# Head norms' sums spread over column tiles, the sparse branch ahead of the memory's, the diagonal first among the level scores, and 38 column tiles computed with 512-column matmuls

## The chip, the cores and the metric

The kernel runs on one core of a Trainium2 chip. The metric is the device time of one execution in microseconds (us), the median of several runs. Every time below is from the profiled execution of the kernel before, unless it is called a run's time.

## The reference

Two transformer blocks follow each other on one sequence of 256 tokens of width 1024, all in float32. Cut to the order of its steps:

```python
# block 1
h = rms_norm(x, norm_mix); proj = h @ w_in             # stick-breaking heads, GLA heads, gates
o_sb = stick_breaking_attention(sb_q, sb_k, sb_v)
o_gla = gla_chunked(g_q, g_k, g_v, log_a)              # gated linear attention, chunks of 64
x = x + (sigmoid(gate_sb) * (o_sb @ w_proj_sb) + sigmoid(gate_gla) * (o_gla @ w_proj_gla)) @ w_out
x = x + square(relu(rms_norm(x, norm_mlp) @ w_ff1)) @ w_ff2
# block 2
proj = rms_norm_2(x, norm_mix_2) @ w_in_2
q, k_s, k_w, qm = (rms_norm_2 of every head)           # the head norms
o_nsa = nsa_attention(...)                             # compressed, selected and window keys
o_m = softmax(qm @ km) @ vm                            # a memory of 256 frames
u = silu(layer_norm(conv31(a * sigmoid(ag))))
merged = g0 * (o_nsa @ w_nsa_out) + g1 * (u @ w_conv_out) + g2 * (o_m @ w_mem_out)
h = x + merged @ w_out_2
out = h + (silu(hn @ w_gate) * (hn @ w_up)) @ w_down   # hn = rms_norm_2(h, norm_ffn_2)
```

## The kernel before

Activations lie transposed: 128 features on the partitions, 256 tokens along a row. A product with a weight matrix goes over *column tiles* of 128 output features and, within one, over *K tiles* of 128 input features; `kt` is the number of K tiles. For float32 accuracy weights and activations are each split into a high and a low half of a type that TensorE takes, and a product is hi·h + hi·l + lo·h (weight half first).

`Stream.prepare` brings eight weight tiles at a time: one 512 KB DMA on SP's queue into `raw` (4 buffers), a cast to `hi` on ACT (L520), a subtraction to `lo` on DVE (L522), with three buffers each for `hi` and `lo`.

`steps_b` (L278) computes column tiles in one of two ways. A *plain* pair of tiles takes for every K tile three matmuls of 256 columns (L324 hi·h, L326 hi·l, L328 lo·h; L308 to L310 are the same for the pair that leads a matrix). A *joint* tile uses that h and l of a K tile lie side by side: for every K tile one matmul of 512 columns gives hi·[h|l] (L295) and one of 256 columns adds lo·h (L296). It fills both halves of a PSUM bank alone, and what evacuates it, called with c = 0, must add the halves. In this kernel wf2, wdn (7 of 8 tiles each) and 40 of the 44 tiles of wgu2 are joint; wgu2's `evf` copies one half on ACT (L1179) and adds the other on DVE (L1180) into `ffr`, and works on a pair at every second tile. wo1, wf1, wo2 and the projections are plain. `residual` (wo1, wo2) adds a tile to x on DVE (L551), splits it (ACT L429, DVE L430) and sums its squares (ACT L462, POOL L469). `evf` of wf1 takes max and scale on DVE (L691), the square on ACT (L693) and splits the result into halves (ACT L426, DVE L427).

Four other places matter.

- `gla_scores` (L744) computes scores within chunks by levels of halving width. In three pairs, six batches of 64 matmuls of 32x32 (L822) are issued: five from a `level` tile `lev` (made on DVE, ACT, DVE, L791 to L794) and, sixth, the diagonal, straight from `gq` and `gk`. A mask per level multiplies them on DVE (L825). They run inside the plain tiles of w1a and the projection `gemm_a` (L367).
- `block_two` (L1043) writes PE's order by hand in a `manual_schedule` (L1098 to L1130). There `compress` (matmuls L1229, L1239, L1258, L1266), `nsa_operands` and the gate column tiles (`fill(gates, ...)`) are generators stepped in turn. `nsa_operands` (L1300) squares the head vectors ksw, q and qm on ACT (L1310) and sums each over a head by matmuls against a column or two of ones (L1313, forty, all in its first step), then makes 1/sqrt by Ln (L1292), Exp (L1293) and one Newton step (L1294 to L1296) and spreads it over rows by matmuls (L1328).
- `w2v` follows as a `gemm_a`: 48 matmuls of 256 columns on L367.
- The branches (L1147 to L1160) run in the order memory (wmo), sparse attention (wno), convolution (wco). Each evacuation multiplies by its gate (L1151) and adds into the gate tiles `gm[4..5]`: branch 0 on POOL, branch 1 on DVE (L1153).

Of the kernel before, what the change touches and what calls it, by code (L numbers as in the profile page):

```python
# [446 lines left out]

class Squares:
# [97 lines left out]
def residual(K, x, H, gain, sqs):  # L546
    nc = K.nc

    def ev(i, c, ps):
        d = x[i // 4][:, (i % 4) * 256:(i % 4 + c) * 256]  # L550
        nc.vector.tensor_tensor(d, ps.rearrange("p a t -> p (a t)"), d, op=OP.add)  # L551
        for j in range(c):
            K.split(H.h(i + j), H.l(i + j), d[:, j * 256:j * 256 + 256], gain[:, i + j:i + j + 1])
        sqs.add(d)
    return ev


def block_one(K, B, after):
# [125 lines left out]
    K.gemm_b(K.stream("wo1"), 8, 8, M, residual(K, x1, X1, par["norm_mlp"], sqs1), lead=nothing, single=2)  # L684
# [11 lines left out]
    K.gemm_b(K.stream("wf1"), 8, 32, X1, evf, lead=lambda: r1.append(K.rms(sqs1.parts(), D, EPS, "rr")[1]))  # L696
# [47 lines left out]
def gla_scores(K, c, gq, gk):  # L744
# [64 lines left out]
    for pr in range(3):  # L809
        ps = K.pt().rearrange("p (l i h t) -> p l i h t", l=2, i=2, h=4)  # L810
        for j in range(2):
            l = 2 * pr + j
# [11 lines left out]
        for j in range(2):  # L824
            nc.vector.tensor_tensor(m[:, j * 256:j * 256 + 256].rearrange("p (a t) -> p a t", t=32),  # L825
                                    ps[:, j].rearrange("p i h t -> p (i h) t"), bc(lv[:, 2 * pr + j], 8), op=OP.mult)
# [216 lines left out]
def block_two(K, B, KM, vm, out):  # L1043
# [54 lines left out]
    with tc.manual_schedule(engines={mybir.EngineType.PE}):  # L1098
# [3 lines left out]
        for _ in range(6):  # L1102
            next(cmp)
            fill(heads, 1)
# [6 lines left out]
        fill(gates, 2)  # L1111
        next(cmp)
        pre = nsa_operands(K, N, B.eps)
# [33 lines left out]
    def branch(n):  # L1147
        def ev(i, c, ps):
            d = slice((i % 4) * 256, (i % 4 + c) * 256)
            g_, t = gm[2 * n + i // 4][:, d], gm[4 + i // 4][:, d]  # L1150
            nc.vector.tensor_tensor(g_, ps.rearrange("p a t -> p (a t)"), g_, op=OP.mult)  # L1151
            if n != 2:
                (nc.vector if n == 1 else nc.gpsimd).tensor_tensor(t, t, g_, op=OP.add)  # L1153
            if n == 1:
                K.split(M.h(i, c), M.l(i, c), t)
        return ev

    K.gemm_b(K.stream("wmo"), 4, 8, OM, branch(2))
    K.gemm_b(K.stream("wno"), 4, 8, ON, branch(0))
# [3 lines left out]
    K.gemm_b(K.stream("wo2"), 8, 8, M, residual(K, B.x, XF, par["norm_ffn"], sqs), lead=nothing, single=2)  # L1163
# [136 lines left out]
def nsa_operands(K, N, eps):  # L1300
# [6 lines left out]
    for x, n, rhs, m in ((ksw, 2, con["mean64"][:, ::64], 2), (q, 4, con["mean64"][:, ::64], 2),  # L1307
# [3 lines left out]
        for t in range(2):  # L1311
            for i in range(n):
                mm(sums[:, t, at + i * m:at + i * m + m], lhsT=sq[:, i * 256 + t * 128:i * 256 + t * 128 + 128],  # L1313
                   rhs=rhs, start=True, stop=True)
        at += n * m
    v, y, w = (K.small(n, [128, 32], bufs=1) for n in ("hn_v", "hn_y", "hn_w"))
# [291 lines left out]
```

## Time and profile before

| what | value |
|---|---|
| runs | 918.21, 918.55, 919.99 us; median 918.55 us |
| profiled execution | 920.02 us, its span 918.2 us |
| mean granted clock of TensorE | 0.991 of full speed |
| busy share: PE, DVE, ACT, POOL | 98%, 74%, 53%, 6% |
| chain that ended last | 94% on PE |
| DMA | 155.64 MB, mean 170 GB/s; 512 KB weights land after about 3.7 us |

The span is the time between the first and the last instruction of the profile. A matmul's end is modelled, so that rates are read from the starts of rows that follow each other: the timeline joins equal instructions and gives the first start, and the next row's start tells when the engine went on.

### The profile page before, as it was taken

The page shows a single profiled execution, that of the slowest core. Times are in us where ns is not written, and L with a number is a line of the kernel's source. Part 1 is how long each engine was busy: PE and PEld are TensorE (multiplying, and loading weights), DVE is VectorE, ACT ScalarE, POOL GpSimd, SP SyncE. Part 2 cuts the span into 40 slices and gives each one's busy share as a digit, 9 for nine tenths or more (in the row PEclk, how much of TensorE's full clock was granted, in tenths as well). Part 3 has the DMA queues.
Part 4 walks back from the last instruction along what each step waited for, and adds up shares of the span by engine and source line. Part 5 has one row for each costly group of instructions (what it writes and reads, how often), then busy time and mean ns, then how long its engine had stood idle before and what let it go on. Part 6 is the DMA issues. An engine that isn't in the chain of part 4 may idle for free.

```text
span 918.2 us, 17035 instructions
## 1 busy us (share of the span) xinstructions
PE 900.6 (98%) x6818; PEld 828.4 (90%) x6818; DVE 675.6 (74%) x1169; ACT 491.1 (53%) x747; POOL 51.1 (6%) x82
## 2 busy tenths in 40 slices
PE   8998999999999999999999999899999999999998
PEld 6987689999999999888899988799999988888887
DVE  6996768866677666555557986899988788888653
ACT  6653764654456555444444434667854565555432
POOL 1000001210020000001120000000003200000000
PEclk9999999999999999999999998999999999999999
DMA  7643426765666666555656762343445566666672
GB/s 274 202 138 117 115 70 184 228 196 174 195 194 196 180 185 186 173 173 185 189 165 186 225 224 75 95 136 118 116 135 164 184 189 186 191 189 185 193 204 64
DMA packets 45727, 155.64 MB, mean 170 GB/s; under 512 B 5200, under 2 KB 6736, under 8 KB 45648
## 3 DMA queue, kind: packets, MB, share of 16 engines
q1 hardware_dynamic: 45216, 153.48, 54.7%
q8 instruction: 53, 0.87, 0.4%
q10 hardware_dynamic: 432, 1.08, 0.4%
q14 instruction: 26, 0.21, 0.1%
HBM read 153.49 MB, written 1.05 MB: 168 GB/s over the span
## 4 chain that ended last, share of the span: by engine, by line
PE 94%; DVE 3%; issue 1%; ACT 1%; DMA 0%; SPq 0%; DVEq 0%
PE pj L295 18%; PE pj L324 17%; PE pj L326 16%; PE pj L328 16%; PE pj L296 9%; PE pj L367 6%; DVE lo L522 1%; PE pj L309 1%; PE pj L310 1%; PE pj L308 1%; ACT hi L520 1%; PE pt L913 1%; PE pt L1313 1%; PE pt L403 1%; PE pt L1229 1%
## 5 line engine op out<-in xcount | busy, mean ns | idle before, releaser
L520 ACT CAST hi<-raw 128x1024 fp32r<-128x1024 f32 (+1 forms) x278 | 288.6, 1041 | 315.7 <-PE pj L326 133.7
L522 DVE TENSOR_TENSOR lo<-raw,hi 128x1024 fp32r<-128x1024 f32 (+1 forms) x278 | 341.3, 1230 | 105.4 <-ACT hi L520 93.4
L295 PE MATMUL pj<-hid,hi 128*128 128x512 f32 x378 | 134.3, 400 | 0.0
L295 PE MATMUL pj<-xf,hi 128*128 128x512 f32 x320 | 113.2, 399 | 0.0
L296 PE MATMUL pj<-hid,lo 128*128 128x256 f32 x378 | 106.2, 281 | 0.0
L296 PE MATMUL pj<-xf,lo 128*128 128x256 f32 x320 | 89.8, 281 | 0.0
L295 PEld LDWEIGHTS pj<-hid,hi 128*128 128x128 f32 x378 | 71.0, 188 | 17.4
L295 PEld LDWEIGHTS pj<-xf,hi 128*128 128x128 f32 x320 | 60.1, 188 | 14.9
L296 PEld LDWEIGHTS pj<-hid,lo 128*128 128x128 f32 x378 | 71.4, 189 | 0.0
L296 PEld LDWEIGHTS pj<-xf,lo 128*128 128x128 f32 x320 | 60.4, 189 | 0.0
L1536 DVE SCALAR_TENSOR_TENSOR cv<-u,par,cv 128x256 f32<-128x256 f32 x120 | 53.2, 479 | 0.7
L324 PE MATMUL pj<-xm,hi 128*128 128x256 f32 x336 | 50.9, 294 | 0.0
L324 PEld LDWEIGHTS pj<-xm,hi 128*128 128x128 f32 x336 | 44.2, 193 | 5.0 <-ACT hi L520 2.5
L326 PE MATMUL pj<-xm,hi 128*128 128x256 f32 x336 | 47.9, 286 | 0.0
L328 PE MATMUL pj<-xm,lo 128*128 128x256 f32 x336 | 47.2, 283 | 0.0
L328 PE MATMUL pj<-xn,lo 128*128 128x256 f32 x304 | 44.8, 286 | 0.0
L469 POOL TENSOR_TENSOR acc<-acc,ffr 128x256 f32<-128x256 f32 (+1 forms) x25 | 27.3, 1103 | 310.4 <-ACT ffr L462 288.9
L326 PEld LDWEIGHTS pj<-xm,hi 128*128 128x128 f32 x336 | 44.1, 195 | 0.0
L326 PE MATMUL pj<-xn,hi 128*128 128x256 f32 x304 | 44.0, 285 | 0.0
L324 PE MATMUL pj<-xn,hi 128*128 128x256 f32 x304 | 43.8, 285 | 0.0
L328 PEld LDWEIGHTS pj<-xm,lo 128*128 128x128 f32 x336 | 43.5, 193 | 0.0
L328 PEld LDWEIGHTS pj<-xn,lo 128*128 128x128 f32 x304 | 39.7, 192 | 0.5 <-issue 0.4
(471 smaller groups left out, 1632.0 us busy)
## 6 DMA issues: line engine op xcount, KB each, us to landing
raw<-in_wf_dram SPq DMA_DIRECT2D x64, 512.0 KB, 3.7
raw<-in_wgu_dram SPq DMA_DIRECT2D x44, 512.0 KB, 3.7
raw<-in_w1g_dram SPq DMA_DIRECT2D x24, 512.0 KB, 3.8
raw<-in_w2g_dram SPq DMA_DIRECT2D x24, 512.0 KB, 3.7
raw<-in_wdn_dram SPq DMA_DIRECT2D x22, 512.0 KB, 3.9
raw<-in_w2a_dram SPq DMA_DIRECT2D x20, 512.0 KB, 3.7
raw<-in_wo_dram SPq DMA_DIRECT2D x16, 512.0 KB, 3.8
raw<-in_w1a_dram SPq DMA_DIRECT2D x14, 512.0 KB, 3.8
```

What stands on the lines that cost most here:

```text
L295: mm(ps, lhsT=st.hi(w), rhs=x.both(k), start=k == 0, stop=False, skip_group_check=True)
L296: mm(ps[:, :T], lhsT=st.lo(w), rhs=x.h(k), start=False, stop=k == kt - 1, skip_group_check=True)
L308: mm(ps[:, j], lhsT=st.hi(w), rhs=x.h(k), start=k + j == 0, stop=False, skip_group_check=True)
L309: mm(ps[:, j], lhsT=st.hi(w), rhs=x.l(k), start=False, stop=False, skip_group_check=True)
L324: mm(ps[:, j], lhsT=st.hi(o + k), rhs=x.h(k), start=k == 0, stop=False)
L326: mm(ps[:, j], lhsT=st.hi(o + k), rhs=x.l(k), start=False, stop=False)
L328: mm(ps[:, j], lhsT=st.lo(o + k), rhs=x.h(k), start=False, stop=k == kt - 1)
L367: mm(pss[t], lhsT=xx(k)[:, t * 128:t * 128 + 128], rhs=ww(o + k), start=k == 0 and xx == x.h and ww == st.hi, stop=k == kt - 1 and ww == s ...
L469: self.engine.tensor_tensor(a, a, s, op=OP.add)
L520: nc.scalar.copy(hi[:, o:o + n], raw[:, o:o + n])
L522: nc.vector.tensor_tensor(lo[:, o:o + n], raw[:, o:o + n], hi[:, o:o + n].bitcast(F32), op=OP.subtract)
L1536: nc.vector.scalar_tensor_tensor(o, u[:, c, k:k + 256], w[:, c, k:k + 1], o, op0=OP.mult, op1=OP.add)
```

## The change

Four edits.

1. wo1 and wo2 (tiles 2 to 6) and wf1 (tiles 2 to 29) become joint: 5 + 5 + 28 = 38 column tiles with 8 K tiles each. wf1's evacuation is wrapped in the new class `Added`; `residual` adds both halves to x, one after the other.
2. In `gla_scores` the diagonal (number 5) becomes the first of the six batches.
3. `nsa_operands` is created ahead of the compression and yields within its sums, so that they are issued in five lots of eight matmuls: after the second, fourth and sixth step of the compression loop, between the first two gate tiles, and at the old place. What follows the sums keeps its place in the code.
4. The branches run in the order wno, wmo, wco; the sums are kept in `gm[0..1]`; branch 0 only multiplies, and branches 2 and 1 add on DVE. POOL adds nothing here any more.

```diff
+class Added:
+    def __init__(self, k, ev):
+        self.k, self.ev = k, ev
+
+    def __call__(self, i, c, ps):
+        if c:
+            return self.ev(i, c, ps)
+        if i % 2 == 0:
+            self.z = self.k.gsmall("ffr", [128, 512]).rearrange("p (a t) -> p a t", a=2)
+        o = self.z[:, i % 2]
+        self.k.nc.scalar.copy(o, ps[:, 1])
+        self.k.nc.vector.tensor_tensor(o, ps[:, 0], o, op=OP.add)
+        if i % 2:
+            self.ev(i - 1, 2, self.z)
...
     def ev(i, c, ps):
+        parts, c = (2, 1) if c == 0 else (1, c)
         d = x[i // 4][:, (i % 4) * 256:(i % 4 + c) * 256]
-        nc.vector.tensor_tensor(d, ps.rearrange("p a t -> p (a t)"), d, op=OP.add)
+        for j in range(parts):
+            nc.vector.tensor_tensor(d, ps[:, j * c:(j + 1) * c].rearrange("p a t -> p (a t)"), d, op=OP.add)
...
-    K.gemm_b(K.stream("wo1"), 8, 8, M, residual(...), lead=nothing, single=2)
+    K.gemm_b(K.stream("wo1"), 8, 8, M, residual(...), lead=nothing, single=2, joint=range(2, 7))
...
-    K.gemm_b(K.stream("wf1"), 8, 32, X1, evf, lead=...)
+    K.gemm_b(K.stream("wf1"), 8, 32, X1, Added(K, evf), joint=range(2, 30), lead=...)
...
-            l = 2 * pr + j
+            l = (5, 0, 1, 2, 3, 4)[2 * pr + j]
...
         cmp = compress(K, kc2, N)
-        for _ in range(6):
+        pre = nsa_operands(K, N, B.eps)
+        for i in range(6):
             next(cmp)
+            if i in (1, 3, 5):
+                next(pre)
             fill(heads, 1)
...
-        fill(gates, 2)
+        fill(gates, 1)
+        next(pre)
+        fill(gates, 1)
         next(cmp)
-        pre = nsa_operands(K, N, B.eps)
         next(pre)
...
-            g_, t = gm[2 * n + i // 4][:, d], gm[4 + i // 4][:, d]
+            g_, t = gm[2 * n + i // 4][:, d], gm[i // 4][:, d]
             nc.vector.tensor_tensor(g_, ps.rearrange("p a t -> p (a t)"), g_, op=OP.mult)
-            if n != 2:
-                (nc.vector if n == 1 else nc.gpsimd).tensor_tensor(t, t, g_, op=OP.add)
+            if n:
+                nc.vector.tensor_tensor(t, t, g_, op=OP.add)
...
+    K.gemm_b(K.stream("wno"), 4, 8, ON, branch(0))
     K.gemm_b(K.stream("wmo"), 4, 8, OM, branch(2))
-    K.gemm_b(K.stream("wno"), 4, 8, ON, branch(0))
     K.gemm_b(K.stream("wco"), 4, 8, UC, branch(1), single=2)
...
# nsa_operands, in the loop over the sums
+            if n == 4 and t == 0:
+                yield
         at += n * m
+        if at < 16:
+            yield
```

The list of instructions shows what a scheduler and the pools make of it. In the fences below a row is one instruction or several alike: line, operation, out<-in, shape, count; the numbers behind the names tell tiles apart.

The first place is PE in `gla_scores`. Before, the last two batches (the second of them the diagonal, from gq and gk) stand directly behind each other, within `gemm_a`:

```order
L822 MATMUL pt_619<-lev_658 32x32 x32
L328 MATMUL pj_965<-xn_118,lo_999 128x256
L367 MATMUL pj_1027<-hi_1031,xn_115 128x512 x4
L367 MATMUL pj_1027<-lo_1032,xn_115 128x512 x2
L367 MATMUL pj_1027<-hi_1049,xn_116 128x512 x4
L367 MATMUL pj_1027<-lo_1050,xn_116 128x512
L367 MATMUL pj_1028<-hi_1031,xn_115 128x512 x4
L367 MATMUL pj_1028<-lo_1032,xn_115 128x512 x2
L367 MATMUL pj_1028<-hi_1049,xn_116 128x512 x3
L822 MATMUL pt_700<-lev_701 32x32 x32
L822 MATMUL pt_700<-gq_147,gk_148 32x32 x32
L367 MATMUL pj_1028<-hi_1049,xn_116 128x512
```

After (L822 is now L844, L804 now L826), the diagonal stands early, behind the first half of the matmuls for the 32-wide level:

```order
L326 MATMUL pj_841<-xn_118,hi_874 128x256
L826 MATMUL pt_520<-lev_514 32x32 x8
L844 MATMUL pt_539<-gq_147,gk_148 32x32 x32
L326 MATMUL pj_841<-xn_118,hi_874 128x256
L328 MATMUL pj_841<-xn_115,lo_875 128x256 x2
L826 MATMUL pt_520<-lev_514 32x32 x8
L328 MATMUL pj_841<-xn_116,lo_875 128x256 x2
L328 MATMUL pj_841<-xn_117,lo_875 128x256 x2
L328 MATMUL pj_841<-xn_118,lo_875 128x256 x2
L324 MATMUL pj_903<-xn_115,hi_906 128x256 x2
L844 MATMUL pt_539<-lev_572 32x32 x32
```

The diagonal's batch moved ahead of all five others; the level batches follow it, the third and the fourth of them two matmuls apart, and the last one stands alone within `gemm_a`.

The second place is PE ahead of w2v. Before, all forty sums (L1313) stand together, in front of w2v (L367):

```order
L328 MATMUL pj_6042<-xm_4415,lo_6076 128x256 x2
L1239 MATMUL pt_6104<-con,P_874_6040 128x2x15 x4
L1313 MATMUL pt_6120<-con,hsq_6121 128x2 x4
L1313 MATMUL pt_6120<-con,hsq_6127 128x2 x8
L1313 MATMUL pt_6120<-con,hsq_6137 128x1 x8
L1117 MATMUL pt_6157<-con,glow_5255 128x24 x2
L367 MATMUL pj_6166<-hi_6170,xm_4412 128x256
```

After (L1239 is now L1267, L1313 now L1341, L1117 now L1144):

```order
L328 MATMUL pj_5894<-xm_4249,lo_5934 128x256 x2
L328 MATMUL pj_5894<-xm_4250,lo_5934 128x256 x2
L1267 MATMUL pt_5962<-con,P_909_5892 128x2x15 x4
L1341 MATMUL pt_5651<-con,hsq_5925 128x1 x4
L1144 MATMUL pt_5992<-con,glow_5090 128x24 x2
L367 MATMUL pj_6001<-hi_6005,xm_4247 128x256
```

Eight of the sums stay in front of w2v; the other four lots of eight now stand between plain tiles ahead of it. ACT at the same place before (L1292 is the Ln on the sums, L1293 the Exp, L520 the casts of weights):

```order
L1234 COPY P_874_6040<-pt_5759 128x512
L520 CAST hi_6200<-raw_6198 128x1024
L520 CAST hi_6280<-raw_6278 128x1024
L520 CAST hi_6325<-raw_6323 128x1024
L1292 ACTIVATE hn_w_6149<-hn_v_6147 128x32
L1284 ACTIVATE gate_6160<-gate_6160 128x48
L1284 ACTIVATE cmp_t_6111<-cmp_t_6111 128x128
L1293 ACTIVATE hn_y_6148<-hn_w_6149 128x32
L520 CAST hi_6384<-raw_6382 128x1024
```

And after (Ln is now L1320, Exp L1321, the casts L538):

```order
L1262 COPY P_909_5892<-pt_5594 128x512
L538 CAST hi_6035<-raw_6033 128x1024
L538 CAST hi_6115<-raw_6113 128x1024
L1320 ACTIVATE hn_w_5984<-hn_v_5982 128x32
L1321 ACTIVATE hn_y_5983<-hn_w_5984 128x32
L1312 ACTIVATE gate_5995<-gate_5995 128x48
L1312 ACTIVATE cmp_t_5969<-cmp_t_5969 128x128
L538 CAST hi_6160<-raw_6158 128x1024
L538 CAST hi_6219<-raw_6217 128x1024
```

One cast fewer stands between the copy and the Ln, and both functions of the head norms are ahead of the third cast.

## Rows read from the trace of the kernel before

**Rows 1.** Page: busy time by engine, the instruction queue, the chain by engine.

```profile
PE 900.6 (98%) x6818; PEld 828.4 (90%) x6818; DVE 675.6 (74%) x1169; ACT 491.1 (53%) x747; POOL 51.1 (6%) x82
...
q8 instruction: 53, 0.87, 0.4%
...
PE 94%; DVE 3%; issue 1%; ACT 1%; DMA 0%; SPq 0%; DVEq 0%
```

**Rows 2.** Timeline of PE in wf1, plain: start, length, instruction, count.

```profile
299.98 1.12 PE L324 MATMUL pj<-x1n,hi 128*128 128x256 f32 x8
...
302.86 1.12 PE L324 MATMUL pj<-x1n,hi 128*128 128x256 f32 x8
```

**Rows 3.** Timeline of PE in wf2, joint.

```profile
393.23 0.40 PE L295 MATMUL pj<-hid,hi 128*128 128x512 f32 x1
...
396.05 0.40 PE L295 MATMUL pj<-hid,hi 128*128 128x512 f32 x1
```

**Rows 4.** Busy time of stretches (wgu2): us, busy by engine, clock, DMA.

```profile
740.00:850.00 110.00, 110.00 (x633) 95.77 (x633) 90.03 (x140) 65.45 (x121) 0.00 (x0) 1.00 0.62 186
```

**Rows 5.** Timeline of DVE in wf1: the first step of a pair's evacuation.

```profile
300.18 0.69 DVE L691 SCALAR_TENSOR_TENSOR ffr<-pj,rr 128x512 f32<-128x512 f32 x1 [1.53 <-PE pj L328]
```

**Rows 6.** Timeline of DVE in wo2: one column tile evacuated alone.

```profile
724.21 0.42 DVE L551 TENSOR_TENSOR x<-pj,x 128x256 f32<-128x256 f32 x1 [0.27 <-PE pj L328]
724.55 1.64 DVE L522 TENSOR_TENSOR lo<-raw,hi 128x1024 fp32r<-128x1024 f32 x1
726.11 0.97 DVE L430 SCALAR_TENSOR_TENSOR xf<-x,par,xf 128x256 fp32r<-128x256 f32 x1
```

**Rows 7.** Timeline of PE in the level scores: two gaps within batches, the projection behind.

```profile
68.51 0.25 PE L822 MATMUL pt<-lev 128*32 128x32 f32 x3 [0.51 <-issue]
...
76.88 0.41 PE L822 MATMUL pt<-gq,gk 128*32 128x32 f32 x25 [2.23 <-issue]
...
78.25 3.39 PE L367 MATMUL pj<-hi,xn 128*128 128x512 f32 x8
81.44 0.85 PE L367 MATMUL pj<-lo,xn 128*128 128x512 f32 x2
```

**Rows 8.** Stretches with the granted clock behind the busy times (columns as Rows 4).

```profile
78.50:82.00 3.50, 3.50 (x10) 2.73 (x9) 3.13 (x6) 0.67 (x2) 0.00 (x0) 0.51 0.25 50
...
546.00:549.50 3.50, 3.50 (x35) 3.50 (x33) 2.63 (x5) 0.49 (x1) 0.00 (x0) 1.00 0.56 150
549.50:559.80 10.30, 10.30 (x50) 10.30 (x51) 2.17 (x10) 1.63 (x5) 0.00 (x0) 0.50 0.13 51
```

**Rows 9.** Timeline of PE around the sums and w2v.

```profile
547.01 6.38 PE L1313 MATMUL pt<-con,hsq 128*128 128x2 f32 x40
553.25 1.03 PE L1117 MATMUL pt<-con,glow 128*128 128x24 f32 x4
554.10 3.76 PE L367 MATMUL pj<-hi,xm 128*128 128x256 f32 x16
...
564.59 0.42 PE L1258 MATMUL pt<-cmp_h,par 128*64 128x16 f32 x8 [2.02 <-DVE hn_y L1296]
```

**Rows 10.** Timelines of ACT and DVE in the same stretch.

```profile
557.90 1.04 ACT L520 CAST hi<-raw 128x1024 fp32r<-128x1024 f32 x1 [11.41 <-PE pj L367]
558.85 0.23 ACT L1292 ACTIVATE hn_w<-hn_v 128x32 f32<-128x32 f32 x1
...
563.02 1.22 DVE L522 TENSOR_TENSOR lo<-raw,hi 128x1024 fp32r<-128x1024 f32 x1 [0.54 <-ACT hi L520]
```

**Rows 11.** Timeline of PE where the compressed keys are scored.

```profile
578.31 1.94 PE L1366 MATMUL pt<-cmp_kn,q 128*128 128x32 f32 x16 [0.46 <-DVE nb L1411]
580.09 1.92 PE L324 MATMUL pj<-xm,hi 128*128 128x256 f32 x8
```

**Rows 12.** Timeline of PE at the start of the branches.

```profile
667.46 1.10 PE L1520 MATMUL pt<-PTm,vm 128*128 128x256 f32 x4 [0.84 <-DVE om L427]
669.02 0.38 PE L324 MATMUL pj<-om,hi 128*128 128x256 f32 x1 [0.46 <-ACT om L426]
```

More of the change, by code (lines that the diff above doesn't have):

```diff
@@ L682, in block_one @@
     sqs1 = Squares(K)
-    K.gemm_b(K.stream("wo1"), 8, 8, M, residual(K, x1, X1, par["norm_mlp"], sqs1), lead=nothing, single=2)
+    K.gemm_b(K.stream("wo1"), 8, 8, M, residual(K, x1, X1, par["norm_mlp"], sqs1), lead=nothing, single=2,
+             joint=range(2, 7))
     K.tap("x1", x1[0])
@@ L694, in evf @@
         K.split(Hd.h(i, c), Hd.l(i, c), r)
-    K.gemm_b(K.stream("wf1"), 8, 32, X1, evf, lead=lambda: r1.append(K.rms(sqs1.parts(), D, EPS, "rr")[1]))
+    K.gemm_b(K.stream("wf1"), 8, 32, X1, Added(K, evf), joint=range(2, 30),
+             lead=lambda: r1.append(K.rms(sqs1.parts(), D, EPS, "rr")[1]))
     B.KM, B.vm = mem()
@@ L825, in gla_scores @@
             nc.vector.tensor_tensor(m[:, j * 256:j * 256 + 256].rearrange("p (a t) -> p a t", t=32),
-                                    ps[:, j].rearrange("p i h t -> p (i h) t"), bc(lv[:, 2 * pr + j], 8), op=OP.mult)
+                                    ps[:, j].rearrange("p i h t -> p (i h) t"), bc(lv[:, (5, 0, 1, 2, 3, 4)[2 * pr + j]], 8), op=OP.mult)
         if pr:
@@ L1162, in block_two @@
     sqs = Squares(K)
-    K.gemm_b(K.stream("wo2"), 8, 8, M, residual(K, B.x, XF, par["norm_ffn"], sqs), lead=nothing, single=2)
+    K.gemm_b(K.stream("wo2"), 8, 8, M, residual(K, B.x, XF, par["norm_ffn"], sqs), lead=nothing, single=2,
+             joint=range(2, 7))
     K.tap("h", B.x[0])
```

## The prediction

> **What bounds the kernel now.** I read the page first, for who is busy and what the last chain consists of: PE is busy 98% of the span, 94% of the chain is PE's, and DVE follows at 74% [rows 1]. A shorter wait elsewhere is therefore worth something only where PE stands still or runs slowly. So I went through PE's timeline for stretches in which rows start further apart than the same rows do elsewhere, and asked the table of stretches for the granted clock there. Three kinds of loss turn up near the edited lines: gaps within a run of equal matmuls for which no releaser but "issue" is named [rows 7]; stretches at half clock, one of them 10 us long while PE is busy throughout [rows 8]; and waits for DVE or ACT [rows 9, 12]. DMA is no limit: PE runs without a gap at 186 GB/s [rows 4].
>
> Price of a step. A plain column tile with eight K tiles is 24 matmuls of 256 columns; in wf1 one such tile goes from 299.98 to 302.86, 2.88 us [rows 2]. A joint tile is eight steps; in wf2 they go from 393.23 to 396.05, 2.82 us [rows 3]. Joint saves 0.06 us per tile, no more.
>
> **Edit 1, joint tiles.** 38 tiles by 0.06 us = 2.3 us off PE, all of it on the path. What it adds lies on DVE and ACT. For a pair of wf1's tiles DVE has two `lo` of 1.22 us [rows 10], two adds of 256 columns at 0.42 [rows 6], the scaling at 0.69 [rows 5] and a split of the same size taken at the same price: 2.44 + 0.84 + 1.38 = 4.66 us of the pair's 5.64. ACT has two casts of 1.04 and at most four more passes, each under the cast. The cover is DVE's rest of 1.0 us per pair. It is enough in wgu2, whose joint tiles do the same sort of work: there DVE is busy 90.0 of 110 us, which is 4.62 per 5.64, and PE 110.0 of 110 [rows 4]. wo1 and wo2 are tighter: `lo`, two adds and the split are 1.22 + 0.84 + 0.48 to 0.97, and `lo` has been seen at 1.64 [rows 6], so 2.5 to 3.45 us against 2.82. In the worst case DVE falls behind by 0.6 us on each of ten tiles; three `lo` buffers take up the first of that. Bounds of edit 1: a gain of 2.6 (rounding) down to a loss of 2; I take 2.3, since nearest to it is wgu2, where none is lost.
>
> By a page of the Trainium skill, "TensorE: Matmul & The Clock Gate", section "Back-to-back issue gap", matmuls in a stream are spaced by their weight loads as well as by themselves, and 512 columns sustain about 131 ns. By that the joint step would shed far more; rows 3 have it at 0.35 us, against 0.36 for the plain step of rows 2, so the trace disagrees.
>
> **Edit 2, the diagonal first.** Two gaps stand inside batches of equal matmuls, 0.51 and 2.23 us, with no engine or DMA named [rows 7]. Both lie where 64 matmuls of a few columns go by in well under a microsecond. By rows 7 and the order of the batches 3 + 1 + 20 + 64 + 39 = 127 matmuls lie between them, with a load each 254 instructions, and the instruction queue moved 0.87 MB in 53 packets [rows 1], one for each 257 of PE's 2 x 6818 instructions: 16 KB each. I read them as PE running out of code because the batches use it up faster than it comes. The second gap is in the diagonal, which stands right behind another batch. Behind it the clock falls: 0.51 from 78.5 to 82 [rows 8], and eight projection matmuls take from 78.25 to 81.44, 3.19 us, where two thirds of a 0.3525 joint step by eight is 1.9; with the next two, 1.5 us. Moved to the front, the diagonal needs no `lev` tile, gq and gk are long there, and no two batches touch any more, though the third and fourth level batches stand only two matmuls apart. Its mask is multiplied early, and DVE's mask of the last level now closes the scores; gla_values reads them several microseconds later, behind gemm_a, so I cost that at nothing. Where a level batch comes forward by its `lev`, it may have to wait for DVE and ACT: 0 to 1 us, I take 0.3, since in the trace no level batch waits. Sum: 0.5 + 2.2 + 1.5 - 0.3 = 3.9 us; bounds 0 (the gaps move along to the close pair) to 4.3. A loss is excluded only as far as no work is added.
>
> **Edit 3, the sums spread.** The clock is full to 549.5 and 0.50 from there to 559.8, though PE is busy 10.3 of 10.3 us [rows 8]. What PE did before it fell were the last eight matmuls of the compression and 24 sums of two columns, 3.3 us without a wide matmul. At half clock fall the end of the sums, the gates' four and w2v. The forty sums take 6.24 us (547.01 to 553.25) [rows 9]; at 0.11 each, as sixteen narrow ones take at full clock (578.31 to 580.09) [rows 11], 4.45: 1.8 lost. The gates' four take 0.85 instead of 0.45: 0.4. w2v's 48 matmuls of 256 columns run from 554.10 to the gap's start at 564.59 - 2.02 = 562.57, 8.47 us; at 0.120 (rows 2) 5.76: 2.7. Together 4.9. After the change lots of eight, 0.9 us each, stand between plain tiles, and only twenty narrow matmuls, about 2.2 us, in front of w2v. The nearest row for a rest of that length speaks to both sides: the sixteen narrow matmuls of rows 11 ran at full clock, but came behind waits, and the tile after them starts at 0.21 per matmul (1.71 us for eight).
>
> Then the wait of 2.02 us for the last head-norm step on DVE [rows 9]. The sums end at 553.25, but Ln starts at 558.85: it stands behind a cast that waits for w2v's own half-clock matmuls until 557.90, and a second `lo` at 563.02 stands between the reciprocal and the last step [rows 10]. In the new order two casts, both with free buffers, stand ahead of Ln; Exp follows directly, and one `lo` fewer comes before the last step. w2v at full clock is 5.76 us; from the last sum the chain is Ln and Exp (0.5), a `lo` that can end some 4.2 us after w2v starts, and two steps behind it: done near 4.7. So the wait goes with about 1 us to spare; what is late next is L1272 and the keys' scores, whose own waits I leave as they are. Four extra switches cost 0.1 us each: 0.4 to 0.8, I take 0.5. Sum: 4.9 + 2.0 - 0.5 = 6.4 us; bounds 1.5 (the clock still falls for w2v, or the wait stays) to 7.
>
> The trace speaks against a rule here: the same page of the Trainium skill, section "HAM oscillation — how this bites in real kernels", has the clock fall through gaps in which PE waits for data. In rows 8 PE was busy without a gap before it fell. By the page the sums' place would not matter to the clock.
>
> **Edit 4, the order of branches.** PE waits 0.84 us for the memory's `om` split, then 0.46 more when wmo reads it [rows 12]. With wno first, whose inputs are long there, a whole first tile (12 matmuls of 0.12) covers both. But wno's third weight block then needs a buffer that the previous matmuls free only just before: 0.6 us for its cast and 0.3 for its `lo`, by the 1.04 and 1.22 of rows 10. Gain 1.3 - 0.9, with POOL's adds gone from beside DVE: 0.5, bounds -1.2 to 1.3. The last merged tile needs four added 0.69 adds on DVE in wmo; they stand within its idle time there.
>
> **Sum.** 2.3 + 3.9 + 6.4 + 0.5 = 13.1 us off a span of 918.2, which gives 905.1. The profiled execution took 920.02, 1.8 more than its span and 1.5 more than the median of the runs; against the median the forecast is 918.55 - 13.1 = 905.4.
>
> **Rivals.**
> (a) The clock still falls around w2v, or the wait behind it stays. For: the 2.2 us rest, and the tile in rows 11. Edit 3 is then worth 1.5 to 4.4 instead of 6.4: 907.4 to 910.3. If only gaps counted, as in the rule above, the clock would fall as before and edit 3 give 2.0 - 0.5: 910.3; one part of this case.
> (b) The code gaps stay and only move, to the close pair of level batches. For: the same count of instructions, and 128 of the 384 still near each other. Edit 2 gives 0 to 1.5: 907.8 to 909.3. The Trainium skill, "Runtime: NRT & Kernel Launch", section "Instruction fetch mechanics", has blocks of 256 instructions, which the spacing agrees with, but calls the crossing mostly hidden; the two gaps of rows 7 are not hidden.
> (c) Weight loads space the matmuls. A joint step has two instead of three, so 0.24 instead of 0.36: 36.5 us less on 304 steps, 918.55 - 36.5 - 10.8 = 871. Rows 3 give 0.3525 with the same two loads, so hardly.
> (d) Slower: `Added` and the second adds make DVE the bound. Place: fourteen pairs of wf1 and ten tiles of wo1 and wo2. It decides from a loss of 13.1 us, e.g. 0.65 us on each of those ten and 0.5 on each pair gives 13.5 and 919; at 0.65 and 0.65, 15.6 and 921. Against: 1.0 us of rest per pair, and wgu2 [rows 4].
> (e) It does not do what it says: gaps and clock loss reappear next door for as much as is saved. Then 918.5 to 916.3 (edit 1 alone).
>
> **How the numbers follow.** The forecast's case holds 903 to 907.4, with chance 0.62; (a) 0.14, (b) 0.13, both together 0.03 (about 912.5), (c) 0.01, (d) 0.03, (e) 0.04. The range takes the forecast's case, (a) and (b): 902.5 to 910.5. Faster by over 0.2% (1.8 us, about what a measurement can tell here) is everything but (d) and half of (e): 0.95; within 0.2%: 0.03; slower: 0.02.
>
> **What would show it.** Plain rows of wf1 replaced by 512-column ones, a tile every 2.82 us, with no wait for DVE or ACT before them; if they wait, (d). No "issue" gap within the level batches and clock 1.00 from 71 to 82; if gaps stay, (b). Clock 1.00 from 540 to 565, w2v in 5.8 us, and no wait for the last head-norm step; if not, (a). The waits of rows 12 gone, with under 1 us for weights instead. The forecast is wrong if the clock falls in a place that has it whole now.

## The result, and the profile after

The changed kernel takes 906.47 us (median of 4 runs, 906.07 to 907.75), the kernel before 919.13 us beside it (4 runs, 918.21 to 919.99). The ratio is 0.9865, with a 95% interval of 0.9848 to 0.9882: 12.7 us less. The profiled execution took 906.7 us, its span 904.9 us; the prediction was 905.4 us, and 905.1 for the span.

The page's first lines, as in [rows 1]:

```profile
PE 890.9 (98%) x6514; PEld 806.0 (89%) x6514; DVE 692.0 (76%) x1215; ACT 497.7 (55%) x779; POOL 44.4 (5%) x82
...
PE 90%; DVE 5%; issue 2%; DMA 1%; ACT 1%; SPq 0%; DVEq 0%; ACTq 0%
```

PE has 304 matmuls fewer, one for each joint step (38 tiles by 8 K tiles), and is 9.7 us less busy.

Where the 13.3 us of the span went is best seen by stages. Each begins with the start of the first matmul of its kind on PE's timeline and ends with that of the next. The level-score stage begins with the profile and ends with the first stick-breaking score. The head-norm stage goes from the first matmul of block 2 to the first score against selected keys; "selection" from there to the first memory output.

| stage | before, us | after, us | difference | forecast |
|---|---|---|---|---|
| level scores | 85.43 | 80.94 | -4.5 | -3.9 |
| wo1 and what leads to it | 46.77 | 46.32 | -0.45 | -0.3 |
| wf1 | 115.63 | 114.53 | -1.1 | -1.7 |
| head norms | 98.46 | 91.74 | -6.7 | -6.4 |
| selection | 52.61 | 53.06 | +0.45 | 0 |
| branches | 38.37 | 37.65 | -0.7 | -0.5 |
| wo2 | 23.04 | 22.77 | -0.3 | -0.3 |

All other stages stand within 0.1 us of each other. PE's timeline in the level scores, where [rows 7] had two gaps (start, length, instruction, count, idle before):

```profile
50.92 0.75 PE L844 MATMUL pt<-gq,gk 128*32 128x32 f32 x61
...
64.03 0.76 PE L844 MATMUL pt<-lev 128*32 128x32 f32 x64
64.72 0.38 PE L328 MATMUL pj<-xn,lo 128*128 128x256 f32 x1
65.19 0.75 PE L844 MATMUL pt<-lev 128*32 128x32 f32 x64
...
72.52 0.76 PE L844 MATMUL pt<-lev 128*32 128x32 f32 x64
73.21 1.43 PE L367 MATMUL pj<-hi,xn 128*128 128x512 f32 x5
...
78.12 1.98 PE L367 MATMUL pj<-hi,xn 128*128 128x512 f32 x8
```

No row has a gap with "issue" ("issue": PE waited for nothing that the profile names) any more; the eight projection matmuls at 78.12 take 1.82 us to the next row (79.94) where [rows 7] had 3.19. Between the close pair of batches, which stand one matmul apart in the trace and not two, one start is late: 64.72 to 65.19 for one matmul of 256 columns, 0.35 us more than its 0.12 (in the five traces of the old order the batch behind such a matmul at 67.3 us starts 0.1 to 0.15 us late). The stretches, with the clock in the third column from the end, as in [rows 8]:

```profile
71.00:78.50 7.50, 7.50 (x94) 5.98 (x94) 6.58 (x11) 3.16 (x3) 0.00 (x0) 1.00 0.53 149
78.50:82.00 3.50, 3.41 (x21) 2.49 (x19) 2.01 (x2) 1.84 (x3) 0.00 (x0) 1.00 0.64 208
544.00:560.00 16.00, 16.00 (x160) 15.57 (x160) 14.84 (x38) 8.47 (x15) 0.00 (x0) 1.00 0.40 135
560.00:568.50 8.50, 6.91 (x50) 6.22 (x50) 7.78 (x32) 6.03 (x16) 0.00 (x0) 0.95 0.48 160
568.50:572.00 3.50, 3.50 (x22) 3.50 (x22) 1.48 (x7) 0.74 (x3) 0.00 (x0) 0.64 0.00 0
```

The clock is whole (1.00, the level of 2.4 GHz) through the last sums and w2v; what is left of half clock (0.50, the level of 1.2 GHz) lies behind the scores of the compressed keys. PE around w2v, as in [rows 9]:

```profile
543.75 0.97 PE L1267 MATMUL pt<-con,P 128*128 128x30 f32 x8
544.56 1.03 PE L1341 MATMUL pt<-con,hsq 128*128 128x1 f32 x8
545.45 0.60 PE L1144 MATMUL pt<-con,glow 128*128 128x24 f32 x4
545.90 2.17 PE L367 MATMUL pj<-hi,xm 128*128 128x256 f32 x16
...
551.84 0.42 PE L1286 MATMUL pt<-cmp_h,par 128*64 128x16 f32 x8
...
565.98 2.09 PE L1398 MATMUL pt<-cmp_kn,q 128*128 128x32 f32 x16 [0.89 <-DVE nb L1443]
```

And ACT, as in [rows 10]:

```profile
546.60 0.23 ACT L1320 ACTIVATE hn_w<-hn_v 128x32 f32<-128x32 f32 x1 [2.57 <-DVE hn_v L1351]
...
548.11 1.05 ACT L538 CAST hi<-raw 128x1024 fp32r<-128x1024 f32 x1 [0.20 <-PE pj L367]
```

w2v goes from 545.90 to 551.84, 5.94 us, and L1286 (before L1258) follows without a wait. Ln runs at 546.60, 2 us behind the start of the last sums, and ahead of the cast that it stood behind. The wait in front of the compressed keys' scores has grown from 0.46 [rows 11] to 0.89 us. In the branches the two waits of [rows 12] are gone and one has come:

```profile
655.14 1.10 PE L1552 MATMUL pt<-PTm,vm 128*128 128x256 f32 x4
...
661.38 0.74 PE L324 MATMUL pj<-om,hi 128*128 128x256 f32 x4 [0.70 <-ACT hi L538]
```

### The profile page after: what moved, and what is told of

Same layout as the page of the kernel before. It is cut to its first block, busy times and chain, and to the rows that moved or that the text cites. A ratio compares the mean times of both kernels' runs of the same rounds, so it can differ in the third digit from the quotient of the medians.

```text
span 904.9 us, 16519 instructions
## 1 busy us (share of the span) xinstructions
PE 890.9 (98%) x6514; PEld 806.0 (89%) x6514; DVE 692.0 (76%) x1215; ACT 497.7 (55%) x779; POOL 44.4 (5%) x82
## 3 DMA queue, kind: packets, MB, share of 16 engines
q10 hardware_dynamic: 432, 1.08, 0.4%
## 4 chain that ended last, share of the span: by engine, by line
PE 90%; DVE 5%; issue 2%; DMA 1%; ACT 1%; SPq 0%; DVEq 0%; ACTq 0%
PE pj L295 25%; PE pj L296 12%; PE pj L324 12%; PE pj L326 12%; PE pj L328 12%; PE pj L367 6%; DVE lo L540 2%; PE pj L309 1%; PE pj L310 1%; PE pj L308 1%; DMA x<-in_x_dram 1%; ACT hi L538 1%; PE pt L935 1%; PE pt L403 1%; PE pt L1341 1%
## 5 line engine op out<-in xcount | busy, mean ns | idle before, releaser
L538 ACT CAST hi<-raw 128x1024 fp32r<-128x1024 f32 (+1 forms) x278 | 288.8, 1042 | 298.8 <-PE pj L326 107.8
L295 PE MATMUL pj<-x1n,hi 128*128 128x512 f32 x224 | 79.3, 399 | 0.0
L296 PE MATMUL pj<-x1n,lo 128*128 128x256 f32 x224 | 62.9, 281 | 0.0
L295 PEld LDWEIGHTS pj<-x1n,hi 128*128 128x128 f32 x224 | 42.1, 188 | 10.3
L324 PE MATMUL pj<-xn,hi 128*128 128x256 f32 x304 | 43.9, 285 | 0.0
```

The lines of the kernel that those rows point to most:

```text
L295: mm(ps, lhsT=st.hi(w), rhs=x.both(k), start=k == 0, stop=False, skip_group_check=True)
L296: mm(ps[:, :T], lhsT=st.lo(w), rhs=x.h(k), start=False, stop=k == kt - 1, skip_group_check=True)
L324: mm(ps[:, j], lhsT=st.hi(o + k), rhs=x.h(k), start=k == 0, stop=False)
L538: nc.scalar.copy(hi[:, o:o + n], raw[:, o:o + n])
```

## The experiments

My theory was that the four edits act apart, each on its own stretch, by the mechanisms of the prediction. Each single edit was put into the kernel before; beside them, on the same chip, 28 runs of before had a median of 916.66 us.

### One edit alone

**e1_joint** is edit 1 alone (the diff of `Added`, `residual` and the three `joint` ranges):

```diff
+    K.gemm_b(K.stream("wf1"), 8, 32, X1, Added(K, evf), joint=range(2, 30), ...)
```

> The kernel before with edit 1 alone (38 joint tiles). Theory: the four edits act on separate stretches and add up. By the stages of the two traces edit 1 gave 0.45 us up to the first wf1 matmul, 1.10 in wf1 and 0.27 in wo2, 1.8 together, and about 0.5 of it was given back because DVE, with two more adds per wo1 tile, is late with the lo that wf1's first tiles read: so about 1.8 us less than before, 0.998 of it, with the wait of 0.4 us for lo behind the first wf1 matmuls here too, and the stretches of the level scores and of w2v unchanged to 0.1 us. Rival: the late lo comes from another edit's shift in time; then no such wait here and 2.3 us less.

Measured: 914.12 us, ratio 0.9967 (0.9954 to 0.998). By stages wo1 took 46.55, wf1 114.31 and wo2 22.77 us: 0.22 + 1.32 + 0.27 = 1.8 us less, as expected. The late `lo` is there as well, though too short for a named wait: behind the fifth matmul of wf1 at 263.98 the next starts at 264.39, 0.41 us later instead of 0.12. The rival falls.

**e2_diag** is edit 2 alone:

```diff
-            l = 2 * pr + j
+            l = (5, 0, 1, 2, 3, 4)[2 * pr + j]
```

> The kernel before with edit 2 alone (the diagonal's batch first). Theory (the gaps and the half clock go with the place of the batches): from the start to the first stick-breaking matmul 4.5 us less, 80.9 instead of 85.4, clock 1.00 from 71 to 82, all later stages unchanged: 0.995 of before. Rival (the gaps are tied to something else at that time, and it was another edit that moved it): the gaps of 0.5 and 2.2 us are here too and the time is that of before.

Measured: 913.75 us, ratio 0.9971 (0.9957 to 0.9985). The level scores end at 81.02 us, with the clock whole:

```profile
71.00:82.00 11.00, 10.95 (x113) 8.51 (x111) 8.59 (x13) 4.91 (x6) 0.00 (x0) 1.00 0.59 178
```

The gain by this stage is 4.4 us against the first trace of before, but the ratio says 1.4 to 3.9. Part of the difference shows in the other kernels that keep the old order of the batches (e1, e3, e4 and, below, e5): their level scores end at 84.73, 83.79, 83.87 and 85.53 us. In e3_sums the gap is the same, and the clock behind it does not fall:

```profile
76.84 0.41 PE L822 MATMUL pt<-gq,gk 128*32 128x32 f32 x25 [2.23 <-issue]
78.23 2.01 PE L367 MATMUL pj<-hi,xn 128*128 128x512 f32 x8
```

The eight matmuls are 2.01 us long, where [rows 7] had 3.39. So the long gap is in every profiled execution of the old order (2.2 to 2.5 us); the short one is 0.2 to 0.55 us long in four of them and missing in e1_joint; and the half clock behind them is in three (before, e1_joint, e5_shift). The edit is worth 2.8 to 4.6 us by stages, 3.8 in the mean of these five against the 80.9 of the new order.

**e3_sums** is edit 3 alone:

```diff
+            if i in (1, 3, 5):
+                next(pre)
...
-        fill(gates, 2)
+        fill(gates, 1)
+        next(pre)
+        fill(gates, 1)
```

> The kernel before with edit 3 alone (the sums in five lots). Theory: 6.7 us less from the first matmul of the second block to the compressed keys (2.2 before w2v, 4.5 in w2v and the wait behind it), and 0.4 us given back at the compressed-key scores, whose wait for DVE grows from 0.46 to 0.9: 6.3 us less, 0.993 of before, clock 1.00 throughout 540 to 565. Rival: the 0.4 us belongs to another edit; then 6.7.

Measured: 912.75 us, ratio 0.9954 (0.9932 to 0.9975). The head norms took 91.42 us, 7.0 less than before, selection 53.03, 0.42 more: 6.6 together, and the clock is whole where expected. By the ratio it is less, 4.2 us (2.3 to 6.2): the profiled execution took 908.43 us where the median is 912.75, and had the quicker of the two step rates (last section) in wf2 and wgu2. The given-back 0.4 us belong to this edit: what comes earlier meets the same chain on DVE and ACT, and the wait for `nb` is 0.9 us here as after. The rival falls.

**e4_order** is edit 4 alone:

```diff
+    K.gemm_b(K.stream("wno"), 4, 8, ON, branch(0))
     K.gemm_b(K.stream("wmo"), 4, 8, OM, branch(2))
-    K.gemm_b(K.stream("wno"), 4, 8, ON, branch(0))
```

> The kernel before with edit 4 alone (wno ahead of wmo, adds on DVE). Theory: 0.7 us less from the first branch matmul to the first wo2 matmul (38.37 to 37.65 us), a wait of 0.7 us for the cast of wmo's first weights in place of those of 0.84 and 0.46 for the memory's output; 0.9992 of before. Rival: the gain comes from POOL's adds that no longer slow DVE; then a variant in which PE's waits at the start of the branches are not what differs, but those in wno and wco.

Measured: 916.48 us, ratio 0.9997 (0.9981 to 1.0012), which tells nothing apart. The stages do: the branches took 36.63 us, 1.7 less. The two waits for the memory's output (0.84 and 0.46), the only ones of PE in the branches of before, are gone, so the rival falls; the wait for wmo's weights that I expected in their place is not there. But wo2 took 23.64, 0.6 more, with this row in it:

```profile
703.12 0.39 PE L309 MATMUL pj<-mrg,hi 128*128 128x256 f32 x1 [0.30 <-DVE mrg L427]
```

DVE works there without a pause from 695.4 to 705.9 us, the four added adds among its work, and is late with the split: the adds I had costed at nothing. So the edit alone gives 1.1 us. With wo2 joint (after) the wait in front of wmo is there and the one for the merged tile is not; in the kernel with wo2 plain below (e7_wf1only) the stages are 36.64 and 23.65 again. So with wo2 plain the order gains 1.1 us, and with wo2 joint 0.7, beside joint's own 0.3; PE's order of the branch tiles differs between the two (after begins wmo at 661.38, ahead of wno's last tiles; e4_order and e7_wf1only do not), and the wait goes with it.

The product of the four ratios is 0.989; for all four at once it is 0.9865 (0.9848 to 0.9882). By stages the single edits give 1.8 + 4.4 + 6.6 + 1.1 = 13.9 us, together 13.3. The medians carry besides what differs between executions of one kernel (the half clock behind the gaps, and the step rates below). The product lies just outside the interval of all four, but has four uncertainties of its own, some 0.003 together: that the edits add up is read from the stages, and the medians neither show nor exclude it.

### The changed kernel again

> The changed kernel again, on the chip of the runs beside it, as their reference. By the product of the four single edits' ratios (0.9967, 0.9971, 0.9954, 0.9997) it is at 0.989 of before if they only add up; by the first runs of the changed kernel at 0.9865. In the profile: no gap in the level scores, clock 1.00 from 71 to 82 and from 540 to 560.

Measured: 906.12 us against 918.45 us, ratio 0.987 (0.9851 to 0.9889). Level scores 80.73, head norms 91.72. wf1 took 113.94, without the late `lo`: exactly 1.69 us less than before, 28 tiles by 0.06. Selection took 54.43, though, 1.8 more than before: the half clock behind the scores of the compressed keys lasts longer there (a stretch of 6.8 us against 3.4 in after).

### The code gap

**e5_shift** adds eight matmuls on zeros, whose result nobody reads (in float32 each is two matmul records with a load each), to those at the very start of the kernel before:

```diff
+            for _ in range(8):
+                nc.tensor.matmul(p[:, :1], lhsT=z[:, :128], rhs=z[:, :1], start=True, stop=True)
```

> The kernel before with eight more one-column matmuls in float32 at its very start, where PE waits for DVE anyway: 16 matmul records, with their loads 32 instructions. Theory (code comes in pieces of 256 instructions, and the batches use it up faster than it comes): the gap in the diagonal's batch moves 16 matmuls earlier in the order, to behind its 23rd instead of its 39th matmul, and the gap of the fourth level batch to behind its 45th instead of its 61st; lengths about as before, 2.2 and 0.5 us. Rival (the gap hangs on data, on PSUM or on the time): it stays behind the 39th matmul.

Measured: one run, 917.25 us. PE's timeline in the level scores:

```profile
67.29 0.59 PE L824 MATMUL pt<-lev 128*32 128x32 f32 x45
68.43 0.38 PE L824 MATMUL pt<-lev 128*32 128x32 f32 x19 [0.55 <-issue]
...
74.21 0.36 PE L824 MATMUL pt<-gq,gk 128*32 128x32 f32 x21
76.86 0.57 PE L824 MATMUL pt<-gq,gk 128*32 128x32 f32 x41 [2.28 <-issue]
```

45 are done and 19 left where it was 61 and 3; 41 are left of the diagonal's 64, so the gap stands behind the 23rd instead of the 39th. In the order of the work it moved by just the 16 records that were put in 70 us earlier; its time hardly changed (68.43 and 76.86 us against 68.51 and 76.88), so this run alone excludes data and PSUM, but not the time. The time is excluded by e1_joint, where the batches came earlier and the long gap with them:

```profile
76.29 0.58 PE L843 MATMUL pt<-gq,gk 128*32 128x32 f32 x25 [2.23 <-issue]
```

Counted from the first matmul record of the trace, the gaps stand behind the 730th and the 857th in all five profiled executions of the old order, e5_shift among them (127 records, which with their loads are 254 instructions): what fixes them is the number of instructions. (In e1_joint the first of the two is a start 0.2 us late and no gap.) The traces also hold the packets of the instruction queue, 16 KB each. One landed within the long gap and one shortly before the short one, and PE went on 1.3 to 1.5 us after it had landed, in all five traces and at both places (before: 67.05 and 75.42 us, PE at 68.51 and 76.88). So PE waited for code. This agrees with the blocks of 256 instructions of the Trainium skill, "Runtime: NRT & Kernel Launch", section "Instruction fetch mechanics"; that crossing them is mostly hidden, which it says too, did not hold at these two places.

A piece of code that begins within a batch is not enough for a gap, though. By the same count one begins in the changed kernel behind the 44th matmul of the last level batch, at 72.92 us, and PE does not stop: that packet had landed at 67.55, 5.4 us ahead. The packets themselves take about 1 us in both orders; in the kernel before, the late one was started 5.7 us behind the beginning of the previous piece on PE (74.25 after 68.51), in the changed kernel 1.1 us behind it (66.49 after 65.36). Why it was started so late no run shows.

### The clock and the sums

**e6_block** puts the forty sums back into one block, in another place of the changed kernel:

```diff
-            if i in (1, 3, 5):
-                next(pre)
...
         fill(gates, 1)
         next(pre)
```

> The changed kernel with the forty sums in one block again, but between the first and the second gate column tile, away from the compression's last matmuls and the gates' four. Theory (the clock falls behind a run of matmuls of one or two columns, 3.3 us long before): the block takes 40 x 0.11 = 4.4 us, the clock falls at its end or in the tile behind it, and what follows at half clock costs 1 to 3.5 us; w2v runs at full clock or just gets it back; 907 to 910 where the changed kernel has 906.1 to 906.5. Rival (what matters is the bunch right in front of w2v, or a wait there): clock 1.00 throughout, time as the changed kernel's.

Measured: 910.14 us, ratio 0.9921 (0.9903 to 0.9938) to before, 4.4 to 4.7 us behind the changed kernel by their distances to before, and just above the 907 to 910 that I had expected. By stages the head norms took 97.81 us, 6.1 more than in the changed kernel; wf1 at the quicker rate (last section) and selection give 1.4 and 1.6 back against after2. The stretches:

```profile
538.00:541.00 3.00, 3.00 (x17) 3.00 (x17) 0.00 (x0) 0.00 (x0) 0.00 (x0) 0.55 0.59 175
541.00:546.00 5.00, 5.00 (x28) 5.00 (x28) 2.16 (x8) 0.80 (x3) 0.00 (x0) 0.59 0.00 0
546.00:549.00 3.00, 2.33 (x20) 2.16 (x20) 2.26 (x6) 0.71 (x1) 0.00 (x0) 1.00 0.00 0
```

And PE's timeline, after the last of the sums:

```profile
542.17 2.05 PE L324 MATMUL pj<-xm,hi 128*128 128x256 f32 x8
...
556.22 0.42 PE L1283 MATMUL pt<-cmp_h,par 128*64 128x16 f32 x8 [1.64 <-DVE cmp_h L1275]
```

The sums start at 535.93 and end at 542.17: 6.24 us, as in [rows 9], instead of 4.45. The clock falls within the block and not at its end, with PE busy for all of the 3.00 us from 538 to 541, and is half in the wide tile behind it (1.86 us for eight matmuls at 542.17, to the next start at 544.03). The fall is thus tied to the block, not to w2v or to a wait: at w2v the clock is whole. The second part of the loss is new: a wait of 1.64 us behind w2v and one of 0.67 within it, both for DVE, but for other tiles than before. So the block costs the clock in this second place too, and waits come back with it. Whether the columns of its matmuls or their number matters, these runs do not tell. The rule of the Trainium skill that I had weighed ("TensorE: Matmul & The Clock Gate", section "HAM oscillation — how this bites in real kernels", gaps in which PE waits for data) explains neither [rows 8] nor this fall; falls of the clock behind waits do exist here too, in e11_dve4 below.

### What the evacuation can bear

**e9_dve** and **e11_dve4** lay two and four more passes of 256 columns on DVE per joint tile of wf1 (they change no value):

```diff
         self.k.nc.vector.tensor_tensor(o, ps[:, 0], o, op=OP.add)
+        self.k.nc.vector.tensor_tensor(o, o, o, op=OP.max)   # twice; four times in e11_dve4
```

> The changed kernel with two more passes of 256 columns on DVE per joint tile of wf1 (the maximum of a tile with itself). Theory: a pair of tiles has 5.64 us, DVE is busy 4.66 of them and would be 4.66 + 4 x 0.42 = 6.34, 0.70 too much; fourteen pairs, the first of them hidden by free buffers: 8 to 10 us longer, all in wf1, which then takes 122 to 124 us instead of 114.5. Rival: the evacuation already holds PE up (a bank or a buffer is the limit, not DVE's busy time); then each added microsecond counts in full, 14 x 1.68 = 23 us. Second rival: there is more room than the busy times say; under 3 us.

Measured: 907.9 us, ratio 0.9881 (0.9857 to 0.9906) to before; wf1 114.82 us, 0.9 more than in the changed kernel beside it. The forecast of 8 to 10 us is wrong; the second rival holds. DVE's timeline says why:

```profile
300.90 0.42 DVE L462 TENSOR_TENSOR ffr<-ffr 128x256 f32<-128x256 f32 x1
301.24 1.23 DVE L542 TENSOR_TENSOR lo<-raw,hi 128x1024 fp32r<-128x1024 f32 x1
302.38 0.42 DVE L463 TENSOR_TENSOR ffr<-ffr 128x256 f32<-128x256 f32 x1
302.72 0.42 DVE L461 TENSOR_TENSOR ffr<-pj,ffr 128x256 f32<-128x256 f32 x1
```

A pass with a duration of 0.42 us is followed 0.34 us after its start, a `lo` of 1.23 after 1.14: the durations of neighbours overlap. (Passes that read what the one before them wrote start 0.45 apart: 302.72, 303.17 and 303.63.) By distances of starts a pair costs 2 x 1.14 + 2 x 0.34 + 2 x 0.61 = 4.2 us of DVE, not the 4.66 of my sum, and with four more passes 5.5, just under the pair's 5.65. The stretch from 300 to 366.84 had DVE busy for 62.87 of 66.84 us, and PE waited once, for 0.7 us.

> The changed kernel with four more passes of 256 columns on DVE per joint tile of wf1 (two in e9_dve, which cost nothing: there the passes started 0.34 us apart, not their 0.42 us of duration, and DVE was busy 62.9 of 66.8 us). Theory: by the distance of starts a pair costs DVE 4.19 us, with eight more passes 4.19 + 8 x 0.34 = 6.9 against 5.65: 1.25 us too much, fourteen pairs, one or two of them hidden: 15 to 17.5 us longer in wf1, 129 to 132 us there. Rival: the evacuation is bounded elsewhere; then under 8 or over 25.

Measured: one run, 933.43 us. wf1 took 141.59 us, 27.6 more than in the changed kernel. The stretch of wf1:

```profile
259.51:401.10 141.59, 124.46 (x696) 108.73 (x695) 122.72 (x231) 68.32 (x105) 2.29 (x3) 0.93 0.49 151
```

And the longest of PE's waits (line, waited for, us in total, times, longest):

```profile
PE pj L295 <- DVE ffr L461: 7.0, 4, 3.4
PE pj L324 <- DVE ffr L461: 5.3, 1, 5.3
```

PE stood still for 141.59 - 124.46 = 17.1 us (0.01 in the changed kernel's wf1), which the theory had at 15 to 17.5. The rest, 10.5 us, is PE being busy longer, and this is mostly the clock: 0.93 in the mean, 7% of 141.59 is 9.9 us; it falls to half behind waits of 2.7 and 3.4 us, and also behind pairs of 1.0 and 0.8 us. The number of the rival (over 25) is reached, but by the clock, not by the evacuation. So the bound is DVE by the distance of its starts, rival (d) has a room of some 1.4 us per pair, and past it, in this one run, each microsecond cost more than one.

### A version that beats both

The wait that grew (0.89) stands among 0.70, 0.48 and 1.08 us in the same stretch. **e8_fill** moves one gate column tile to the front of it:

```diff
     first(0)
-    fill(gates, 1)
+    fill(gates, 2)
     first(1)
...
-        if i < 2:
+        if i < 1:
             fill(gates, 1)
```

> The changed kernel with one more gate column tile between the first and the second head's selected-key scores, and one fewer at the end of the second round of the four. Theory: the waits of 0.70, 0.89, 0.48 and 1.08 us there all come from chains that are late by less than a tile's 2.88 us; they go, and with them the half clock behind them (1.5 us): 3 to 4.6 us less, about 902.5 to 903.5 where the changed kernel has 906.5. Rival: the waits are only pushed to the place that has a tile less, and the time stays within 0.5 us.

Measured: 901.74 us, ratio 0.9813 (0.9792 to 0.9834) to before, 4.4 us under the changed kernel beside it. PE's timeline in e8_fill:

```profile
565.67 0.87 PE L1432 MATMUL pt<-ks,qs 128*128 128x256 f32 x4
566.38 1.87 PE L1398 MATMUL pt<-cmp_kn,q 128*128 128x32 f32 x16
568.09 1.20 PE L324 MATMUL pj<-xm,hi 128*128 128x256 f32 x8
```

The stretch from w2v to the branches, in e8_fill and then in the changed kernel beside it:

```profile
545.00:652.00 107.00, 105.84 (x865) 98.88 (x865) 101.11 (x293) 78.22 (x171) 0.00 (x0) 1.00 0.40 124
```

```profile
545.00:657.00 112.00, 108.58 (x859) 101.29 (x860) 101.82 (x294) 78.85 (x171) 0.00 (x0) 0.97 0.37 118
```

The waits in front of L1432, L1398 and L1462 (3.2 us in the changed kernel beside it) are down to two of 0.15 and 0.28 us, one of 0.7 us for the weighted scores (L1419) is new, and the clock is whole through the stretch. The rival falls. From the first score against selected keys to the first branch matmul it is 88.9 us, where the changed kernel had 93.5 in its first profiled execution and 94.8 in the one beside it: 4.5 to 5.9 us less.

**e7_wf1only** takes `joint` from wo1 and wo2 again, and **e10_both** does so in e8_fill:

```diff
-    K.gemm_b(K.stream("wo1"), ..., single=2, joint=range(2, 7))
+    K.gemm_b(K.stream("wo1"), ..., single=2)
```

> The changed kernel with wo1 and wo2 plain again; only wf1 is joint. Theory: two more adds per tile keep DVE busy to the end of wo1, so the lo that wf1's second K tile reads comes late, 0.5 us. Without them that matmul waits for nothing and wf1 takes 0.5 us less, about 114.0 us from its first matmul to wf2's; wo1 and wo2 take 0.3 to 0.45 and 0.27 more. In sum within 0.3 us of the changed kernel. Rival: the late lo is a matter of the casts or of the DMA; then it is there as before, and the time is 0.7 us longer.

Measured: 906.64 us, ratio 0.9864 (0.9844 to 0.9884): the time of the changed kernel, within 0.5 us. wf1 took 112.52 us, 1.4 less than with wo1 joint, but not for want of a late `lo`, which the changed kernel beside it did not have either: every joint tile of wf1 takes 2.77 us instead of 2.83. Rows of wf1 in e7_wf1only, then in the changed kernel beside it:

```profile
300.19 0.39 PE L295 MATMUL pj<-x1n,hi 128*128 128x512 f32 x1
300.42 0.28 PE L296 MATMUL pj<-x1n,lo 128*128 128x256 f32 x1
300.54 0.39 PE L295 MATMUL pj<-x1n,hi 128*128 128x512 f32 x1
...
302.97 0.39 PE L295 MATMUL pj<-x1n,hi 128*128 128x512 f32 x1
```

```profile
299.98 0.40 PE L295 MATMUL pj<-x1n,hi 128*128 128x512 f32 x1
...
302.81 0.40 PE L295 MATMUL pj<-x1n,hi 128*128 128x512 f32 x1
```

Whether the late `lo` hangs on wo1's adds is thus not settled by this run: of all profiled executions it is in two of the seven with wo1 joint (after, e1_joint) and in none of the seven with wo1 plain.

> The one more gate tile of e8_fill together with wo1 and wo2 plain as in e7_wf1only. In e7_wf1only wf1's joint tiles went 2.77 us apart in the profiled execution, in the changed kernel 2.83. If that is set by the program, wf1 takes 112.5 us here too; if by chance of the execution, it can be 114.0. Time: e8_fill's 901.7 less 0 to 1.4.

Measured: 900.98 us, ratio 0.9821 (0.9804 to 0.9837), the same as e8_fill's. wf1 took 112.52 us again. It is not set by wo1, though: e6_block, with wo1 joint, has 112.56.

## Why the prediction was right, point by point

- **The whole.** 905.4 us forecast, 906.5 measured; the span 905.1 forecast, 904.9 measured. The terms were 2.3, 3.9, 6.4 and 0.5; by stages they came to 1.8, 4.5, 6.3 (6.7 less 0.45 given back) and 0.7. Errors of -0.5, +0.6, -0.1 and +0.2 cancelled; that the sum came out within 0.2 us of the span is luck, since profiled executions of one kernel already differ by more (selection 53.06 and 54.43 us in the changed kernel).
- **Edit 1.** The price of 0.06 us per tile is right where nothing disturbs it (wf1 in after2: 1.69 for 28 tiles). The lower end I had set for wo1 showed itself, but in one matmul and not in ten tiles: in two executions (after and e1_joint) the `lo` came late there, and wf1 began with a loss of 0.4 to 0.6 us. The cover in wf1 was larger than I had worked out, since I had added durations that overlap (4.66 us for 4.2).
- **The rule on weight loads** in a stream (the Trainium skill, "TensorE: Matmul & The Clock Gate", section "Back-to-back issue gap") does not hold here: a joint step is 0.346 or 0.353 us in every trace, so rival (c) is out.
- **Edit 2.** Place, cause and size of the gaps were right: PE waited for code. That the batches use it up faster than it comes is only half of it: in the new order a piece begins within a batch too, but its packet came in time. The close pair of batches, on which rival (b) stood, costs 0.35 us, and by the count of instructions no piece begins there. The half clock behind the gap was put down as a fixed 1.5 us. It is there in some executions only (before, e1, e5: level scores of 84.7 to 85.5 us) and not in others (e3, e4: 83.8 to 83.9), so this term is 0 to 1.5.
- **Edit 3.** Both parts were right, the clock (w2v in 5.94 us, forecast 5.76 to 5.8) and the wait of 2.02 us. That the remaining bunch of twenty narrow matmuls keeps the clock was a choice between two sides; it does in all eight profiled executions of kernels with the five lots. What I left as it was, the wait in front of the compressed keys' scores, grew by 0.43 us.
- **Edit 4.** The sum of 0.5 us was near (0.7), but its parts were not all where I had them: the wait of 0.6 us for a cast, which I had put at wno's third weight block, was found as 0.70 in front of wmo's first, and with wo2 plain it is not there at all. Costing the adds on DVE at nothing was wrong in the arrangement with wo2 plain: 0.6 us in wo2.

## What to carry to other kernels

Before a gap is put down to data, count the instructions up to it: where the count and not the work or the time fixes it, PE waits for code, and moving or parting batches of short instructions can take the gap away. The times of the instruction queue's packets tell whether it did. A block of matmuls of a few columns costs more than its own time when the clock falls in it; handed out in small lots between wide tiles, the same work cost hardly more than its own length (the wide tile behind a lot took 2.96 us instead of 2.88). A chain that was late by less than a tile was repaired by one tile moved in front of it, and the stretch is to be looked at again after each edit, because what came earlier waits at the next chain.

## What the runs showed of the hardware that I had not expected

Joint steps go at two rates, 0.346 and 0.353 us, with the same code and at full clock. Undisturbed, a whole matrix keeps one rate, from behind its first three or four joint tiles to its last. wgu2's stage was 123.37 us in e2_diag, e3_sums and e8_fill and 125.4 in the others, wf2's 92.6 in e3_sums and e5_shift and 94.0 in the others, wf1's, where joint, 112.5 in e6, e7 and e10 and 113.9 to 114.8 in the rest without e11_dve4; in wo1 the changed kernel had 2.77 us per tile in one execution and 2.83 in the other. In e9_dve wf1 changed its rate on the way: 2.83 us per tile until two steps at 328 us took 0.05 and 0.07 us longer than the others, 2.77 behind them. So a stream can go over from one rate to the other; what chooses the rate is open and was not tried. It is worth 2 us in wgu2 alone, as much as all of edit 1, and so of the size by which executions of one kernel differ; it is also in part of what single profiled executions show (e8_fill's, at 899.84 us, had the quicker rate in wgu2).
